# Retention's output projection: gate blocks added by accumulating transfers, output weights split at other places, weight sums copied through another queue

## The chip, the cores and the metric

The kernel runs on one core of one Trainium2 chip. The number that counts is the time of one execution on the device, in microseconds (us), lower is better. Each version is run several times and the median is taken; one more execution is recorded by the hardware profiler. The engines are called PE (TensorE: matmuls, with PEld for its weight loads), DVE (VectorE), ACT (ScalarE), POOL (GpSimd) and SP (SyncE, which here only issues transfers).

## The reference

One layer of a hybrid diffusion backbone on 1024 latent tokens of width 1024, with 256 context tokens. An input projection feeds a neighbourhood attention and a bidirectional retention; both are projected back, merged by sigmoid gates, projected once more, and a gated MLP with a depthwise convolution follows. What matters here:

```python
def _merge(o_na, o_ret, gate_na, gate_ret, w_proj_na, w_proj_ret, w_out):
    merged = jax.nn.sigmoid(gate_na) * (o_na @ w_proj_na) + jax.nn.sigmoid(gate_ret) * (o_ret @ w_proj_ret)
    return merged @ w_out
...
        x = x + g1 * _merge(o_na, o_ret, xga, xgb, w_proj_na[l], w_proj_ret[l], w_out[l])
        hx2 = _modulate(_rmsnorm(x, norm2_g[l]), sh2, sc2)
        x = x + g2 * _conv_ffn(hx2, w_up[l], conv_w[l], conv_b[l], w_down[l])
```

All numbers are fp32. w_up has 1024 x 5632 numbers, w_down 2816 x 1024.

## The kernel before

**Products.** An fp32 product is made of three matmuls on reduced-precision operands. Each operand is split into a high part, a copy by ACT (L95), and a low part, a subtraction by DVE (L96): what `split` does. A "block" is 128 x 512 numbers. Large products go by a scheme with seven products of half-size matrices in place of eight (`Seven`), for which sums and differences of weight blocks are needed. `block_sums` (L555) makes them ahead of time in DRAM: for each job four copies from DRAM to DRAM (`copy_of`, L562 in the profile) and four transfers that add onto the destination (`sum_of`, through `add`, L558 in the profile). All are issued by POOL, a few at a time: `puts` lets POOL read one number of a given tile, so that it waits for a place in the work, and then issues the next n items. Sums that were not made ahead (for up's units from `PRE` on) are made by POOL when the unit is loaded: four additions of two blocks, L1431 to L1434 in `Seven.load`.

**Stages**, in the profiled execution: attention to 400 us; retention 400 to 738 (a loop over heads and chunks, `slot`); gate products 738 to 891; the retention's projection 891 to 975; output tiles 975 to 1077; the opening of up 1077 to 1140; up with its convolution to 1500; down to the end. Most of the order is chosen by a scheduler that ships with the language. Written by hand are the parts inside `tc.manual_schedule()`, and single instructions fixed to their place by `late`. All engines work through their own instructions in order.

**The projection** (L1791 on) runs over q = 0 to 27: seven products p of four column blocks n, q = 4p + n, 12 matmuls each. In step q the program issues loads (weights two steps ahead with `w_load`, operands `x_load`, output weights `wo_load`, old products and gates `merge_load`), the block's matmuls, the evacuation of block q - 1, the splitting of weights for q + 2 (`w_split`, tile wc), of operands (`x_split`, tile xop), of output weights (tiles wo, wx or wc), and merges. A finished block is multiplied by its gate on DVE (`merged`, L1717), and POOL adds the other branch's gated product (L1718), which SP loaded from d_pn into a tile of its own. `merge` then splits the sum into mh (ACT) and ml (DVE); for the first row half in steps 10 to 13 and 18 to 21, for the second in the loop over output tiles.

**The output tiles**: `out_proj(tb)` for eight row blocks tb, each two halves dh of 48 matmuls with the split weights `wo[kb, dh]` (eight blocks kb), evacuated by DVE in two instructions (L1844, L1845), then normalized. In the projection's steps 2 to 9 the eight weight blocks of dh = 0 were split, in steps 24 to 27 six of dh = 1; two more follow behind it.

**SP's queue** has eight lanes; a transfer waits, by a semaphore of the program, until the one eight places ahead has landed. POOL's transfers go through its own queue.

Of the kernel before, what the change touches and what calls it, by code (L numbers as in the profile page):

```python
# [40 lines left out]
def tile_hybrid_layer(ctx, tc: tile.TileContext, io, dbg=None):  # L41
# [510 lines left out]
    NH, EARLY, PRE = NF // 2, 4, 4  # L552
    seq = [j + NH * i for j in range(NH) for i in range(2)]

    def block_sums(jobs):  # L555
# [4 lines left out]
        def copy_of(n, c):  # L560
            d, x, y, z, w = jobs[n]
            late(pool.dma_start(d[c], (y, z, z, w)[c]))  # L562
# [750 lines left out]
    def slot(main, mix, head=None, i=None):  # L1313
# [57 lines left out]
    for it in (tl, gate_sums):  # L1371
# [277 lines left out]
    def w_load(p, n):  # L1649
# [5 lines left out]
        if n % 2 == 0 or (p, n) == (0, 1):  # L1655
# [12 lines left out]
    for n, (i, k) in enumerate(steps):  # L1668
        gu[i].step(k)
        if k in (1, 2, 3):  # L1670
            puts(pret_sums if n < 40 else up_sums, (gu[i].u3 if k == 3 else gu[i].u2)[:, 0:1], 2)
        if n in marks:
# [5 lines left out]
            for n_ in {4: (0, 1), 5: (2,)}.get(m, ()):  # L1678
# [26 lines left out]
    def merge_load(db, half):  # L1705
        sg[db, half] = t = [gtile(half, F32, "sg") for _ in range(2)]
        sync.dma_start(t[0], d_pn[db, half])
        sync.dma_start(t[1], d_gate[2 * db + 1, half])

    def merge_gate(db, half):  # L1710
        t = sg[db, half][1]
# [3 lines left out]
    def merged(db, half, src):  # L1715
        s_, g = sg[db, half]
        vec.tensor_tensor(g, src, g, ALU.mult)  # L1717
        pool.tensor_tensor(g, g, s_, ALU.add)  # L1718
# [3 lines left out]
    def merge(db, half):  # L1722
        g = sg[db, half][1]
        mg[db, half] = h_, l_ = gtile(half, F32R, "mh"), gtile(half, F32R, "ml")
        split(h_, l_, g)
# [3 lines left out]
    def wo_load(kb, dh=0):  # L1729
        woraw[kb, dh] = raw = gtile(1, F32, "wr") if dh == 0 else wpool.tile([P, 512], F32, tag="raw", bufs=3, name="raw")  # L1730
        sync.dma_start(raw, io["w_out"][dh, kb])

    def wo_split(kb, dh=0):
        if dh == 0:
            wo[kb, dh] = t = wop.tile([P, 2, 512], F32R, tag="wo", bufs=KB, name="wo")
        else:
            wo[kb, dh] = t = wop.tile([P, 2, 512], F32R, tag="wx", bufs=2, name="wx") if kb >= 6 else wtile()
        split(t[:, 0], t[:, 1], woraw.pop((kb, dh)))
# [7 lines left out]
    WO = {2 + kb: kb for kb in range(KB)}  # L1746
    WX = {24: (6,), 25: (7,), 26: (0, 1), 27: (2, 3)}
    WX_LOAD = {22: (6,), 23: (7,), 24: (0, 1), 25: (2,), 26: (3,)}
    NQ = 7 * KH

    def loads(q):
        if q in XS:
            x_load(*XS[q], lambda: gtile(1, F32, "xr"))
        if 3 <= q + 2 < NQ:
            w_load(*divmod(q + 2, KH))
        if q in WO:
            wo_load(WO[q])

# [32 lines left out]
    with tc.manual_schedule():  # L1791
        for q in (1, 2):
            loads(q)
        for q in range(NQ + 1):
# [4 lines left out]
            for kb in WX_LOAD.get(q, ()):  # L1799
                wo_load(kb, 1)  # L1800
# [10 lines left out]
            if q in WO:  # L1811
                wo_split(WO[q])
            for kb in WX.get(q, ()):
                wo_split(kb, 1)
# [3 lines left out]
            for q0, b in ((10, 0), (18, KH)):  # L1818
# [13 lines left out]
    def out_proj(tb):  # L1832
        half, ts = tb // 4, slice((tb % 4) * P, (tb % 4 + 1) * P)
        x1 = op.tile([P, D], F32, tag="x1", bufs=3, name="x1")
        xr = op.tile([P, D], F32, tag="xn", bufs=2, name="xn")
        sync.dma_start(x1, io["x"][tb * P : (tb + 1) * P])
        for dh in range(2):
            cs = slice(dh * 512, dh * 512 + 512)
            m = po.tile([P, 512], F32, tag="o", bufs=2, name="om")
            for kb in range(KB):  # L1840
                wc = wo[kb, dh]
                h_, l_ = mg[kb, half]
                mm3(m, h_[:, ts], l_[:, ts], wc[:, 0], wc[:, 1], kb == 0, kb == KB - 1)
            vec.tensor_tensor(xr[:, cs], m, gate1[:, cs], ALU.mult)  # L1844
            vec.tensor_tensor(x1[:, cs], xr[:, cs], x1[:, cs], ALU.add)  # L1845
# [6 lines left out]
        return xr  # L1852

# [215 lines left out]
    with tc.manual_schedule():  # L2069
        for kb in (4, 5):  # L2070
# [415 lines left out]
```

## Time and profile before

| what | value |
|---|---|
| median of three runs | 1724.77 us (1721.01 to 1727.42) |
| profiled execution | 1728.52 us, of which the span 1726.8 us |
| PE busy in the span | 1695.7 us, 98% |
| DVE / ACT / POOL busy | 74% / 49% / 37% |
| mean granted clock of PE | 0.995 |
| transfers | 346.11 MB, mean 200 GB/s |

The span runs from the first to the last instruction of the profile; the execution's own time has a little around it. A matmul counts as busy while it is in the pipeline, so PE's share is no measure of how near it is to its best; the number of matmuls in a stretch says more. The rows of the page that show where time is spent evenly and where not (40 slices of 43.2 us each; 9 is 90% or more):

```profile
PE   9999999999999999999999899999999999999998
DVE  5777786665877877567569956798899998846756
POOL 2112234323344333024322321056666666421444
DMA  9256779853352533899988566856766776998744
```

PE dips below nine tenths in the 23rd slice (950 to 993 us); DVE is at nine tenths there and in the slice before.

### The profile page before, as it was taken

The numbers are of one execution on the slowest core, as the hardware profiler recorded it, in microseconds if no ns is written. First come the engines' busy times: TensorE is split into PE (matmuls) and PEld (weight loads), VectorE is DVE, ScalarE is ACT, GpSimd is POOL, SyncE is SP. The second block draws the span as 40 slices with busy tenths as digits, with TensorE's granted clock in tenths as the row PEclk, the third lists the DMA queues.
The fourth block names the chain that finished last, engine by engine and source line by source line (L and its number), as shares of the span: only waits on it lengthen the run. The fifth ranks groups of instructions, "written<-read, shape, count | busy, mean of one in ns | idle before, by whom it ended". The sixth has DMA issues, their size and how long they took to land.

```text
span 1726.8 us, 25317 instructions
## 1 busy us (share of the span) xinstructions
PE 1695.7 (98%) x8365; PEld 1414.2 (82%) x8365; DVE 1283.1 (74%) x2481; ACT 842.0 (49%) x1777; POOL 633.2 (37%) x805
## 2 busy tenths in 40 slices
PE   9999999999999999999999899999999999999998
PEld 7788888888888887888888687778888888888886
DVE  5777786665877877567569956798899998846756
ACT  6565665553453444443455433644444444544444
POOL 2112234323344333024322321056666666421444
PEclk9999999999999999999999999999999999999999
DMA  9256779853352533899988566856766776998744
GB/s 378 92 152 161 179 199 240 202 129 91 81 157 79 171 62 109 286 305 333 281 255 305 181 204 192 286 166 193 194 171 173 197 203 167 266 316 287 244 155 175
DMA packets 168451, 346.11 MB, mean 200 GB/s; under 512 B 29952, under 2 KB 46880, under 8 KB 161728
## 3 DMA queue, kind: packets, MB, share of 16 engines
q1 hardware_dynamic: 132464, 243.45, 41.6%
q0 software_dynamic: 21248, 86.10, 23.2%
q10 hardware_dynamic: 14608, 14.95, 2.5%
q8 instruction: 66, 1.08, 0.2%
q14 instruction: 65, 0.53, 0.1%
HBM read 268.08 MB, written 141.87 MB: 237 GB/s over the span
## 4 chain that ended last, share of the span: by engine, by line
PE 50%; DVE 6%; issue 6%; POOL 3%; DMA 3%; ACT 1%; SPq 0%; POOLq 0%; DVEq 0%; ACTq 0%
PE u L1422 30%; PE y L1422 3%; PE pr L1422 2%; PE mm L132 1%; PE mm L131 1%; PE mm L130 1%; DVE wc L96 1%; PE om L130 1%; PE om L132 1%; PE om L131 1%; DMA ur<-d_a 1%; PE pn L119 1%; PE pn L120 1%; PE pn L121 1%; PE mm L1422 1%
## 5 line engine op out<-in xcount | busy, mean ns | idle before, releaser
L1422 PE MATMUL u<-T,wc 128*128 128x512 f32 x1056 | 248.0, 391 | 3.5 <-DVE pu L1469 3.3
L1422 PEld LDWEIGHTS u<-T,wc 128*128 128x128 f32 x1056 | 199.1, 189 | 46.2 <-issue 2.6
L1422 PE MATMUL y<-wc,ahl 128*128 128x512 f32 (+1 forms) x936 | 210.4, 387 | 0.7 <-DVE wc L96 0.7
L1422 PEld LDWEIGHTS y<-wc,ahl 128*128 128x128 f32 x936 | 174.1, 188 | 37.0 <-DVE wc L96 1.4
L96 DVE TENSOR_TENSOR wc<-ur,wc 128x512 fp32r<-128x512 f32 x155 | 118.1, 765 | 45.6 <-ACT wc L95 43.8
L95 ACT CAST wc<-ur 128x512 fp32r<-128x512 f32 x155 | 95.5, 621 | 92.1 <-PE y L1422 44.9
L1422 PE MATMUL u<-h2a,wc 128*128 128x512 f32 x504 | 118.6, 390 | 1.1 <-ACT pu L1930 1.1
L120 PE MATMUL mm<-low,wc 128*128 128x512 f32 (+1 forms) x312 | 119.2, 382 | 0.0
L1422 PEld LDWEIGHTS u<-h2a,wc 128*128 128x128 f32 x504 | 94.8, 188 | 21.1 <-ACT pu L1930 1.5
L534 POOL DMA_DIRECT2D d_ona<-rs x32 | 32.7, 1023 | 208.7 <-DVE st L495 65.5
L119 PE MATMUL mm<-hx,wc 128*128 128x512 f32 x264 | 107.4, 407 | 0.3 <-ACT hc L233 0.3
L121 PE MATMUL mm<-hx,wc 128*128 128x512 f32 x264 | 105.0, 398 | 0.0
L1422 PE MATMUL u<-hxT,wc 128*128 128x512 f32 x384 | 90.0, 389 | 0.0
L95 ACT CAST wc<-s 128x512 fp32r<-128x512 f32 x72 | 44.8, 622 | 85.7 <-PE u L1422 83.5
L1422 PEld LDWEIGHTS u<-hxT,wc 128*128 128x128 f32 x384 | 72.1, 188 | 14.9
L593 POOL COPY pad<-pu 128x1 f32<-128x1 f32 x62 | 39.3, 633 | 91.9 <-DVE pu L1463 76.8
L96 DVE TENSOR_TENSOR wc<-s,wc 128x512 fp32r<-128x512 f32 x72 | 69.3, 963 | 0.7 <-ACT wc L95 0.3
L96 DVE TENSOR_TENSOR ahl<-ur,ahl 128x512 fp32r<-128x512 f32 x66 | 52.5, 802 | 23.2 <-ACT ahl L95 22.9
L132 PE MATMUL mm<-wc,low 128*128 128x512 f32 (+1 forms) x180 | 68.9, 383 | 0.0
L95 ACT CAST wc<-wr 128x512 fp32r<-128x512 f32 x69 | 42.5, 619 | 53.3 <-PE u L1422 39.4
L1422 PE MATMUL pr<-xop,wc 128*128 128x512 f32 x264 | 63.4, 399 | 4.6 <-DVE xop L96 2.9
L120 PEld LDWEIGHTS mm<-low,wc 128*128 128x128 f32 x312 | 59.2, 190 | 7.2
(441 smaller groups left out, 4724.5 us busy)
## 6 DMA issues: line engine op xcount, KB each, us to landing
ur<-in_w_up SPq DMA_DIRECT2D x80, 256.0 KB, 5.2
d_a<-at SPq DMA_DIRECT2D x77, 256.0 KB, 3.1
ur<-d_a SPq DMA_DIRECT2D x77, 256.0 KB, 5.3
d_w<-in_w_down POOLq DMA_DIRECT2D x66, 256.0 KB, 7.3
aw<-in_w_ada SPq DMA_DIRECT2D x32, 512.0 KB, 4.4
d_a<-d_a POOLq DMA_DIRECT2D x44, 256.0 KB, 7.3
ur<-d_w SPq DMA_DIRECT2D x44, 256.0 KB, 3.6
ur<-in_w_down SPq DMA_DIRECT2D x33, 256.0 KB, 5.5
```

What stands on the lines that cost most here:

```text
L95: act.copy(hi, src)
L96: (lo_eng or vec).tensor_tensor(lo, src, hi.bitcast(F32), ALU.subtract)
L119: pe.matmul(out, wh, xh, start=k == 0, stop=False)
L120: pe.matmul(out, wh, xl, start=False, stop=False)
L121: pe.matmul(out, wl, xh, start=False, stop=k == n - 1)
L130: pe.matmul(out, ah, bh, start=first, stop=False)
L131: pe.matmul(out, ah, bl, start=False, stop=False)
L132: pe.matmul(out, al, bh, start=False, stop=last)
L534: late(pool.dma_start(o, self.rs[HD:P], accum_op=ALU.add))
L593: late(pool.tensor_copy(tick, src))
L1422: pe.matmul(out, a, b, start=first and n == 0, stop=last and n == 2, skip_group_check=True)
```

## The change

Five things are done.

1. `block_sums`: the copies are issued by SP's queue; the accumulating transfers stay on POOL.
2. The sums of the retention projection's weights (d_p) are issued in the retention, one item in each slot, in place of the gate products; those of up (d_s) take all places of the gate products. `PRE` goes from 4 to 8, so eight of up's units get sums in DRAM and load seven blocks each.
3. `merged` adds the old product with a transfer from d_pn that accumulates into the gate's tile, issued by POOL. The separate load of d_pn is gone. Merges of the first half move two steps later; merges of the second half are fixed to their place in the loop over output tiles, in the order of blocks 4 to 7, then 0 to 3.
4. First-half output weights are split in steps 1 to 5 and 25 to 27. All second-half ones are split behind the first and second output products, which now run as (tile 0, first half), (tile 1, first half), then the second halves of both.
5. One weight block of the first product is loaded earlier, and all four of them go to the same kind of buffer.

The diff, cut to its core:

```diff
-    NH, EARLY, PRE = NF // 2, 4, 4
+    NH, EARLY, PRE = NF // 2, 4, 8
...
         def copy_of(n, c):
-            late(pool.dma_start(d[c], (y, z, z, w)[c]))
+            late(sync.dma_start(d[c], (y, z, z, w)[c]))
...
                     puts(gate_sums, head.r0[i][:, 1, 0:1], n)
+                next(pret_sums, None)
...
-            puts(pret_sums if n < 40 else up_sums, (gu[i].u3 if k == 3 else gu[i].u2)[:, 0:1], 2)
+            puts(up_sums, (gu[i].u3 if k == 3 else gu[i].u2)[:, 0:1], 2)
...
     def merge_load(db, half):
-        sg[db, half] = t = [gtile(half, F32, "sg") for _ in range(2)]
-        sync.dma_start(t[0], d_pn[db, half])
-        sync.dma_start(t[1], d_gate[2 * db + 1, half])
+        sg[db, half] = t = gtile(half, F32, "sg")
+        sync.dma_start(t, d_gate[2 * db + 1, half])
...
     def merged(db, half, src):
         vec.tensor_tensor(g, src, g, ALU.mult)
-        pool.tensor_tensor(g, g, s_, ALU.add)
+        pool.dma_start(g, d_pn[db, half], accum_op=ALU.add, max_dma_last_dim=8192)
...
-    WO = {2 + kb: kb for kb in range(KB)}
-    WX = {24: (6,), 25: (7,), 26: (0, 1), 27: (2, 3)}
+    WO = {1: (0,), 2: (1,), 3: (2,), 4: (3,), 5: (4,), 25: (5,), 26: (6,), 27: (7,)}
...
-            for q0, b in ((10, 0), (18, KH)):
+            for q0, b in ((12, 0), (20, KH)):
                 if 0 <= q - q0 < KH:
                     merge(b + q - q0, 0)
...
+        out_begin(1)
+        evacuated(NQ - 1)
...
+        m = out_mm(0, 0)
+        for kb in range(5):
+            wx_split(kb)
+        out_evac(0, 0, m)
+        m = out_mm(1, 0)
+        for kb in range(5, KB):
+            wx_split(kb)
+        out_evac(1, 0, m)
+        for tb in (0, 1):
+            out_half(tb, 1)
...
-        for kb in range(2 * tb, min(2 * tb + 2, KB)):
+        for kb in ((4, 5), (6, 7), (0, 1), (2, 3))[tb] if tb < KH else ():
             merge(kb, 1)
```

`out_begin`, `out_mm`, `out_evac` and `out_end` are the pieces of the former `out_proj`; for tiles 2 to 7 they run in the former order.

**DVE at the end of the projection.** Before, in the last four steps (L96 is the low part of a split, L1788 the evacuation, L1717 the multiplication by the gate):

```order
L96 TENSOR_TENSOR wc<-raw,wc 128x512
L96 TENSOR_TENSOR wx<-raw,wx 128x512
L1788 TENSOR_TENSOR u_10435<-u_10435,pr 128x512
L1717 TENSOR_TENSOR sg<-u_10435,sg 128x512
L96 TENSOR_TENSOR wc<-wr,wc 128x512
L96 TENSOR_TENSOR wx<-raw,wx 128x512
L1788 TENSOR_TENSOR u_10468<-u_10468,pr 128x512
L1717 TENSOR_TENSOR sg<-u_10468,sg 128x512
L96 TENSOR_TENSOR wc<-raw,wc 128x512 x2
L1788 TENSOR_TENSOR u_10501<-u_10501,pr 128x512
L96 TENSOR_TENSOR ml<-sg,mh 128x512
L1717 TENSOR_TENSOR sg<-u_10501,sg 128x512
```

After, from step 25 to the first output tile's evacuation (there L1785 is the evacuation, L1846 the output tile's):

```order
L1785 TENSOR_TENSOR u_10497<-u_10497,pr 128x512
L1717 TENSOR_TENSOR sg<-u_10497,sg 128x512
L96 TENSOR_TENSOR wo<-wr,wo 128x512
L1785 TENSOR_TENSOR u_10525<-u_10525,pr 128x512
L1717 TENSOR_TENSOR sg<-u_10525,sg 128x512
L96 TENSOR_TENSOR wo<-wr,wo 128x512
L1785 TENSOR_TENSOR u_10552<-u_10552,pr 128x512
L1717 TENSOR_TENSOR sg<-u_10552,sg 128x512
L96 TENSOR_TENSOR wc<-raw,wc 128x512 x3
L96 TENSOR_TENSOR wc<-wr,wc 128x512
L96 TENSOR_TENSOR wx<-wr,wx 128x512
L1846 TENSOR_TENSOR xn<-om,gate_10306 128x512
```

The splits of second-half output weights (wx, wc from raw) stood among the last evacuations and now stand behind the last; merges of the second half (ml) are gone from this place.

**POOL at the start of up.** Before, with the sums of an up unit:

```order
L2053 TENSOR_TENSOR zs<-zs,pu 128x512 x2
L1431 TENSOR_TENSOR s<-ur 128x512
L1432 TENSOR_TENSOR s<-s,ur 128x512
L1433 TENSOR_TENSOR s<-ur 128x512
L1434 TENSOR_TENSOR s<-ur,s 128x512
L593 COPY pad<-pu 128x1
L562 DMA d_w<-in_w_down 16x4096 x2
L1981 DMA d_a<-d_a 32x2048
```

After, where the first such sums stand several units later, among the accumulating transfers for down:

```order
L558 DMA d_w<-in_w_down 32x2048
L1993 DMA d_a<-d_a 32x2048
L593 COPY pad<-pu 128x1
L558 DMA d_w<-d_w 32x2048
L1993 DMA d_a<-d_a 32x2048
L593 COPY pad<-pu 128x1
L558 DMA d_w<-in_w_down 32x2048
L1993 DMA d_a<-d_a 32x2048
L1432 TENSOR_TENSOR s<-ur 128x512
L1433 TENSOR_TENSOR s<-s,ur 128x512
```

Four units' sums are gone from POOL's row, and the copies for down (L562) with them.

**SP in the gate products.** Before, loads of gate weights (wr) and of the projection's (raw):

```order
L1508 DMA wr<-in_w_rg 128x512
L1508 DMA wr<-d_g 128x512 x2
L1533 DMA o<-d_oret 128x512 x2
L1508 DMA wr<-d_g 128x512
L1508 DMA wr<-in_w_rg 128x512 x2
```

After, at the same place, with copies of up's weight blocks (L562) among them:

```order
L1509 DMA wr<-in_w_rg 128x512
L1509 DMA wr<-d_g 128x512 x2
L562 DMA d_s<-in_w_up 16x4096 x4
L1534 DMA o<-d_oret 128x512
L562 DMA d_s<-in_w_up 16x4096
L1534 DMA o<-d_oret 128x512
L562 DMA d_s<-in_w_up 16x4096 x2
L1509 DMA wr<-d_g 128x512
L1509 DMA wr<-in_w_rg 128x512
```

Seven copies went in between two weight loads here.

More of the change, by code (lines that the diff above doesn't have):

```diff
@@ L1793, in tile_hybrid_layer @@
             loads(q)
-        for q in range(NQ + 1):
+        for q in range(NQ):
             for q0, b, half in ((5, 0, 0), (13, KH, 0), (18, KH, 1), (23, 0, 1)):
@@ L1810, in tile_hybrid_layer @@
                 x_split(*XS[q])
[L1811 to L1814, printed above, removed]
+            for kb in WO.get(q, ()):
+                wo_split(kb)
             for q0, half in ((8, 0), (24, 1)):
@@ L1852, in out_proj @@
         return xr
+    def out_proj(tb):
+        if tb > 1:
+            out_begin(tb)
+            for dh in range(2):
+                out_half(tb, dh)
+        return out_end(tb)
     vos = {}
```

86 lines of the change are left out of this document (47 added, 39 removed).

## The prediction

> **What bounds the kernel now.** I read the page first: TensorE (PE) is busy 98% of the span, so a change can pay only where PE is not busy, or busy at a lower clock. The windows of 20 us say where that is (columns: stretch, length, busy time and count of PE, PEld, DVE, ACT, POOL, granted clock, DMA share, GB/s):
>
> ```profile
> 920.00:940.00 20.00, 20.00 (x89) 16.54 (x89) 19.97 (x29) 9.33 (x18) 5.61 (x4) 1.00 0.86 286
> 940.00:960.00 20.00, 18.27 (x79) 14.49 (x78) 19.83 (x23) 8.37 (x15) 8.75 (x6) 1.00 0.52 179
> 960.00:980.00 20.00, 17.11 (x67) 13.32 (x66) 19.72 (x23) 8.21 (x15) 8.53 (x6) 0.91 0.58 182
> 980.00:1000.00 20.00, 17.92 (x71) 13.91 (x70) 13.55 (x21) 5.71 (x10) 4.54 (x6) 0.91 0.68 221
> 1120.00:1140.00 20.00, 20.00 (x90) 16.57 (x89) 19.96 (x25) 13.20 (x17) 1.62 (x1) 1.00 0.66 220
> 1140.00:1160.00 20.00, 17.03 (x74) 13.44 (x72) 19.60 (x20) 6.98 (x10) 17.49 (x12) 1.00 0.47 145
> 1160.00:1180.00 20.00, 19.64 (x80) 16.12 (x81) 19.16 (x20) 8.83 (x12) 13.26 (x13) 0.91 0.63 171
> ```
>
> A full window holds 90 matmuls. The retention projection and the first output tiles (940 to 1000) ran 79, 67 and 71, so 53 are missing; the up projection's start (1140 to 1180) ran 74 and 80, so 26 are missing. In all five VectorE (DVE) is the engine that is full, until the projection ends inside the third. What one matmul is worth comes from the chain of work that ended last, in a stretch without waits:
>
> ```profile
> 891.43 10.88 PE pr L1422 x48
> ```
>
> 10.88 / 48 = 0.2267 us. The first loss is 53 x 0.2267 = **12.0 us**, the second 26 x 0.2267 = **5.9 us**, together 17.9 us. Both hold a dip of the clock: the matmuls that ran slow are counted as missing, so the dip must not be added again.
>
> Why DVE is full there, from the groups of instructions by form, 890 to 1000 us (count | busy us, mean ns):
>
> ```profile
> L1718 POOL TENSOR_TENSOR sg<-sg 128x512 f32<-128x512 f32 x16 | 26.2, 1636 | 63.0 <-DVE sg L1717 33.1 <-DMA xr<-d_rt 24.1 <-DMA wr<-d_p 2.0
> L96 DVE TENSOR_TENSOR xop<-xr,xop 128x512 fp32r<-128x512 f32 x16 | 19.6, 1228 | 0.0
> L96 DVE TENSOR_TENSOR ml<-sg,mh 128x512 fp32r<-128x512 f32 x16 | 14.0, 888 | 0.2
> L96 DVE TENSOR_TENSOR wc<-raw,wc 128x512 fp32r<-128x512 f32 x18 | 13.2, 744 | 2.3 <-ACT wc L95 2.3
> L96 DVE TENSOR_TENSOR wc<-wr,wc 128x512 fp32r<-128x512 f32 x13 | 8.9, 683 | 2.1 <-ACT wc L95 1.8 <-DMA raw<-in_w_pret 0.3
> L96 DVE TENSOR_TENSOR wx<-raw,wx 128x512 fp32r<-128x512 f32 x4 | 6.0, 1503 | 0.0
> L96 DVE TENSOR_TENSOR xop<-row,xop 128x512 fp32r<-128x512 f32 x4 | 3.8, 960 | 0.0
> ```
>
> One subtraction of this shape takes 0.68 us where nothing disturbs it (wc from wr), and up to 1.50 on average elsewhere. The timeline shows beside what (start, length, instruction, idle before it):
>
> ```profile
> 962.11 0.68 DVE L96 TENSOR_TENSOR wc<-wr,wc 128x512 fp32r<-128x512 f32 x1
> 962.33 1.59 POOL L1718 TENSOR_TENSOR sg<-sg 128x512 f32<-128x512 f32 x1 [2.01 <-DVE sg L1717]
> 962.71 1.76 DVE L96 TENSOR_TENSOR xop<-xr,xop 128x512 fp32r<-128x512 f32 x1
> 964.52 7.83 PE L1422 MATMUL pr<-xop,wc 128*128 128x512 f32 x26 [2.63 <-DVE xop L96]
> ```
>
> The subtraction that meets POOL's addition L1718 ends about when that does plus its own time, and PE has by then waited 2.63 us. Summed over the groups, the time above 0.68 us is 8.8 (xop from xr), 3.3 (ml), 1.2 (wc from raw), 3.3 (wx) and 1.1 (xop from row): **17.7 us of stretch**, for 16 additions.
>
> **The change part by part.** The sum goes against the profiled execution (1728.52 us, span 1726.8), which lies 3.75 us above the median of the three runs, 1724.77; I carry the difference over to the median.
>
> *The projection.* Windows by stage, in the columns above:
>
> ```profile
> 400.00:738.00 338.00, 336.81 (x1725) 285.70 (x1724) 244.33 (x743) 150.80 (x403) 115.24 (x181) 1.00 0.47 134
> 738.00:891.00 153.00, 153.00 (x675) 126.45 (x674) 95.07 (x148) 63.59 (x106) 51.98 (x95) 1.00 0.90 286
> 891.00:988.00 97.00, 90.67 (x386) 72.89 (x385) 89.00 (x116) 50.49 (x92) 26.73 (x17) 0.98 0.78 270
> ```
>
> DVE has 89.0 us of work, PE 28 blocks of 12 matmuls, 28 x 12 x 0.2267 = 76.2 us: DVE is the bound by about what is lost. The change takes away POOL's additions, with them 17.7 us, and 17 instructions from DVE's row ahead of the first output tile's evacuation (eight splits of the output weights' second half, one of the first, eight splits of merged rows of half 1; five of the output splits come back behind the last block), 17 x 0.68 = 11.6 us. Left for the blocks are 89.0 - 17.7 - 11.6 = 59.7 us, 78% of PE's 76.2. The last blocks, densest before, have five instructions each (3.4 us at 0.68, of 2.72 a block) only while operands of the seventh product are split beside a merge, in the four blocks q = 20 to 23; DVE falls behind there by 4 x 0.7 = 2.7 us, and weights are split two blocks (5.4 us) ahead. So DVE stops being the bound.
>
> What comes in its place is a wait: ACT's copy into mh now waits for a transfer that adds in DRAM's old product. Between a block's multiply and its merge lie three blocks, 3 x 2.72 = 8.2 us. An accumulating transfer into SBUF does not occur in the trace. The nearest are POOL's copies and additions in DRAM (KB each, median us to landing) and POOL's time for one issue:
>
> ```profile
> d_g<-d_g POOLq DMA_DIRECT2D x16, 256.0 KB, 4.3
> d_a<-d_a POOLq DMA_DIRECT2D x44, 256.0 KB, 7.3
> L558 POOL DMA_DIRECT2D d_s<-d_s x8 | 7.3, 918 | 5.5 <-DMA d_s<-d_s 5.3 <-issue 0.3
> L1058 POOL DMA_DIRECT2D d_b<-low x16 | 21.1, 1431 | 4.5 <-issue 4.5
> L562 POOL DMA_DIRECT2D d_s<-in_w_up x16 | 10.0, 628 | 0.3 <-issue 0.2
> ```
>
> That bounds it between 0.6 + 4.3 = 4.9 and 1.4 + 7.3 = 8.7 us. I take 6.5, the middle. Even 8.7 is only 0.5 late, and behind the waiting copy on ACT stand weight splits that PE needs two blocks later; with DVE 2.7 us behind they have 5.4 - 2.7 = 2.7 us to spare. The wait costs PE nothing up to 8.2 + 2.7 = 10.9 us. Also gone are 16 loads of d_pn from SP's queue.
>
> The second half's eight output splits now stand behind tile (0,0). The product after the first two tiles needs them 48 x 0.2267 = 10.9 us after the first began, and each takes ACT 0.62 and DVE 0.68, so eight take some 5.4, or 8.7 us with the two tiles' four instructions of evacuation (2.8) and a start delay of 0.5; hidden. If that cover failed, the wait would be 1 to 3 us. I leave **0.8 us** for the seam, where before 1.9 us of wait was. Projection: **-12.0 + 0.8 = -11.2** (bounds: -12.0, and -4.8 if the stretch stays, below).
>
> *The start of up.*
>
> ```profile
> 1139.44 1.27 DVE L1962 SCALAR_TENSOR_TENSOR at<-uu,cw,at 128x1023 f32<-128x1023 f32 x1
> 1140.24 2.22 POOL L1431 TENSOR_TENSOR s<-ur 128x512 f32<-128x512 f32 x1 [15.51 <-DMA ur<-in_w_up]
> 1141.24 2.31 DVE L1963 SCALAR_TENSOR_TENSOR at<-uu,cw,at 128x1023 f32<-128x1023 f32 x1
> ```
>
> The four sums L1431 to L1434 begin at 1140.24, the moment PE begins to lose. With eight units prepared by transfer instead of four, four units' sums, 16 additions of about 2 us, go from POOL, and a convolution step beside them falls from 2.31 towards 1.27. DVE was full from 1120 already with PE at x90, so it keeps up narrowly without them: I take **-5.0** of the 5.9 (bounds 0 and -5.9). The 32 extra transfers in DRAM run while up's weights are not yet wanted.
>
> *Retention.* It gets pret's 16 accumulating issues (0.92 us each, 14.7 us) on a POOL busy 115 of 338 us, and loses the issue of 16 gate copies there. PE's dependence on POOL in that stage is small:
>
> ```profile
> PE Q L131 <- POOL SS L1231: 1.0, 4, 0.5
> ```
>
> If every added issue delayed a product by its whole length, that would be 14.7 us; if none, 0. PE waited four times, 0.5 us at the longest, so I stay near the lower end: **+0.5**.
>
> *Gate stage and later.* SP issues the copies, which leaves bytes and destinations as they were; PE is at 153.00 of 153.00 there. I take 0 (bounds 0 and the +24 below).
>
> **Sum:** -11.2 - 5.0 + 0.5 = -15.7; 1728.5 - 15.7 = 1712.8 for a profiled execution, and 1724.77 - 15.7 = **1709 us** for the median.
>
> **The rivals.**
>
> *The stretch stays.* A POOL transfer needs POOL to write it out, and if that slowed DVE as the addition did, 17.7 us would stay and only 11.6 of 29.3 go: 12.0 x 0.40 = 4.8 instead of 11.2, so **1715**. Against it:
>
> ```profile
> 1053.22 0.82 POOL L558 DMA_DIRECT2D d_s<-in_w_up  x1
> 1053.36 0.68 DVE L1886 TENSOR_TENSOR vo<-vo,v 128x512 f32<-128x512 f32 x1
> ```
>
> A DVE addition inside such an issue takes its 0.68.
>
> *Late accumulation.* Landing after 10.9 us in the two groups of merges (q = 12 to 15, 20 to 23) would stop ACT, the weight splits behind it and PE. By the wait of 2.63 above and the dip behind it, granted clock 0.91 over the 20 us at 960, so 0.09 x 20 = 1.8 us, a group costs 4.4:
>
> ```profile
> 966.00:968.00 2.00, 2.00 (x6) 1.53 (x6) 2.00 (x2) 0.00 (x0) 1.53 (x1) 0.50 0.26 61
> ```
>
> (In these 2 us behind the wait the clock was 0.50 and 6 matmuls ran.) Two groups: 1709 + 8.8 = **1718**. For it: landings reach 7.3 as a median, with a DMA share of 0.86 at 920 to 940. The Trainium skill ("SBUF — State Buffer", section "SBUF: two separate sides") gives a rule against this change: a transfer issued from GpSimd's queue starves while VectorE runs an operation that holds the port pair both share, and the advice is to issue it from another engine's queue. By it the accumulates would land later and this rival would hold. Its section "Who interferes with whom" counts a tensor_tensor as not doing so, by inference; the 0.68 beside 0.82 above agrees, and I leave the chance where the rows put it. On the dip the skill ("TensorE: Matmul & The Clock Gate", section "What's actually happening") says the clock halves after an idle window of about 3.4 us; here it was 0.50 behind 2.63 us, so the measurement decides; by the page the rival would cost 2 x 2.6 and give 1714.
>
> *Up stays bound by DVE.* DVE was full at 1120 to 1140 without POOL. If the added load of transfers or DVE's own order keeps PE waiting, the 5.0 is not had: 1709 + 5 = **1714**.
>
> *SP's queue becomes serial*, slower than before. The program lets SP have eight transfers under way, each waiting for its predecessor in the same lane. A copy in DRAM takes about 7 us:
>
> ```profile
> d_p<-in_w_pret POOLq DMA_DIRECT2D x24, 256.0 KB, 7.0
> ```
>
> So it costs the queue 7.0 / 8 = 0.9 us, and the 27 copies that SP gets in the gate stage 24 us, ahead of weight loads that PE needs; the DMA share is 0.90 there already. It decides once SP is behind by more than the loads' lead, some 6 us. Then 1709 + 24 = **1733**. Against it: PE waits for nothing there, and the loads are issued early.
>
> **Chances.** Forecast 1709: 0.60; stretch 1715: 0.07; late accumulation 1718: 0.13; up at 1714: 0.12; SP 1733: 0.08. The range takes in all of the 17.9 us with 4 us of other waits and 3 us of spread (the runs shown lie within 4 us of their median), so 1700, and above it the rivals but SP's: **1700 to 1722**. Within 0.5%, about what a measurement of this kernel can tell from no change, is 1716.1 to 1733.4: faster 0.77, same 0.17 (two thirds of late accumulation, a fourth of the others, a fourth of SP's), slower 0.06.
>
> **What would show it.** Right: windows of x90 from 940 to 1000; no L1718 addition on POOL, and xop's and ml's splits near 0.68; DVE below 80% of the projection; ACT's mh waiting for the transfer under 3 us and PE not at all; no L1431 sums before about 1215, and the clock at 1.00. Wrong: PE waiting for mh's or wc's splits behind that transfer (late accumulation), splits of 1.7 beside POOL's issues (the stretch), PE or ACT waiting for wr or raw at 738 to 891 (SP), DVE at 20 of 20 with PE under x85 at 1140 to 1180 (up). A loss in retention over 2 us would break the term of 0.5.

## The result and the profile after

The changed kernel takes **1711.83 us** (median of four runs, 1710.48 to 1713.06), the kernel before 1724.09 in the runs beside it (1721.01 to 1727.42): a ratio of **0.9928, interval 0.9907 to 0.9950**. The profiled execution took 1713.02 us, its span is 1710.8 us.

First the windows that showed the losses, in the changed kernel (columns as in the prediction):

```profile
940.00:960.00 20.00, 20.00 (x90) 16.57 (x89) 18.29 (x30) 9.37 (x17) 6.08 (x7) 1.00 0.96 233
960.00:980.00 20.00, 20.00 (x90) 16.53 (x90) 15.71 (x26) 6.75 (x11) 4.35 (x5) 1.00 1.06 303
980.00:1000.00 20.00, 20.00 (x93) 16.55 (x92) 13.38 (x29) 7.90 (x16) 4.58 (x7) 1.00 0.65 176
1060.00:1080.00 20.00, 20.00 (x97) 16.67 (x96) 17.17 (x39) 12.02 (x28) 0.54 (x1) 1.00 0.77 266
1080.00:1100.00 20.00, 19.80 (x87) 16.07 (x86) 15.71 (x25) 15.97 (x30) 1.62 (x1) 1.00 0.89 302
1140.00:1160.00 20.00, 20.00 (x90) 16.57 (x89) 15.43 (x20) 9.77 (x15) 3.59 (x5) 1.00 0.87 222
1160.00:1180.00 20.00, 20.00 (x90) 16.55 (x89) 14.49 (x18) 9.23 (x13) 4.67 (x6) 1.00 0.80 220
1520.00:1540.00 20.00, 18.54 (x82) 15.02 (x80) 4.86 (x8) 5.42 (x11) 3.13 (x4) 1.00 0.64 149
1540.00:1560.00 20.00, 15.89 (x60) 12.64 (x61) 12.76 (x19) 11.65 (x21) 3.72 (x4) 0.83 0.98 345
```

Both losses are gone: 90 matmuls and more in every window from 940 to 1000 and from 1140 to 1180, at full clock. And a new one has come, where in the kernel before the windows from 1520 to 1560 held 90: at the start of the down projection 8 + 30 = 38 matmuls are missing, 38 x 0.2267 = 8.6 us. The waits of PE name it; three lines of all of them in the changed kernel (who waits, for whom, us in total, times, longest), the last two from the retention:

```profile
PE y L1423 <- ACT wc L95: 5.6, 1, 5.6
...
PE Q L131 <- POOL SS L1231: 1.2, 4, 0.5
PE dS L132 <- DVE kz L1200: 1.0, 2, 0.6
```

The groups of the projection, 884 to 992 us, changed kernel:

```profile
L1718 POOL DMA_DIRECT2D sg<-d_pn x16 | 14.0, 874 | 62.2 <-DVE sg L1717 30.8 <-DVE wc L96 14.2 <-issue 13.6
...
L96 DVE TENSOR_TENSOR xop<-xr,xop 128x512 fp32r<-128x512 f32 x16 | 10.9, 684 | 0.0
```

The split of xop is back at 0.684 us from 1.228, beside POOL issues of 0.87 us. The window of the whole projection shows that VectorE is no longer the bound, with 60.99 of 77 us:

```profile
891.00:968.00 77.00, 77.00 (x342) 63.75 (x341) 60.99 (x97) 41.45 (x78) 12.81 (x15) 1.00 0.97 290
```

To compare whole stages I use the start of the first matmul of each. For instance, the down projection's, from the view of the tile y (ns shortest/median/longest, first and last start), ahead the kernel before:

```profile
L1422 PE MATMUL y<-wc,ahl x936: 278/389/497, 1507.5 to 1718.3; 128*128 128x512 f32 x183, 128*128 128x256 f32 x5
```

and after:

```profile
L1423 PE MATMUL y<-wc,ahl x936: 277/389/792, 1484.0 to 1702.4; 128*128 128x512 f32 x183, 128*128 128x256 f32 x5
```

PE comes to the down projection 23.5 us earlier and takes 7.6 us longer over it. All kernels of this study in the same manner, us from first matmul to first matmul (down: first to last start), one profile each, with the ratio to the kernel before and its interval:

| kernel | retention | gates | projection | output tiles | up | down | median | ratio |
|---|---|---|---|---|---|---|---|---|
| before | 308.7 | 149.6 | 83.6 | 100.6 | 432.0 | 210.8 | 1724.09 | |
| before, second profile (e9) | 309.0 | 149.6 | 82.0 | 98.0 | 430.4 | 210.1 | 1723.97 | 0.9991 [0.9973, 1.0009] |
| accumulation alone (e7) | 309.1 | 149.6 | 76.2 | 103.1 | 429.1 | 210.3 | 1722.11 | 0.9996 [0.9983, 1.0010] |
| output weights alone (e10) | 309.2 | 149.6 | 81.5 | 96.6 | 431.0 | 210.3 | 1719.30 | 0.9969 [0.9953, 0.9986] |
| both edits of the projection (e11) | 309.5 | 149.6 | 76.1 | 94.7 | 429.4 | 210.9 | 1712.91 | 0.9927 [0.9905, 0.9950] |
| ... and copies on SP (e5) | 307.5 | 149.6 | 76.2 | 94.7 | 427.4 | 217.9 | 1717.83 | 0.9970 [0.9958, 0.9981] |
| ... and pret sums in retention (e4) | 310.9 | 149.6 | 76.1 | 94.7 | 426.7 | 215.7 | 1717.06 | 0.9960 [0.9945, 0.9976] |
| ... and eight units: the change | 310.8 | 149.6 | 76.1 | 94.8 | 420.8 | 218.4 | 1711.83 | 0.9928 [0.9907, 0.9950] |
| the change, down's copies on POOL (e1) | 310.3 | 149.6 | 76.1 | 94.7 | 420.8 | 210.3 | 1704.65 | 0.9898 [0.9877, 0.9919] |

From e11 to the change each row adds one edit to the row above ("pret sums" are the weight sums of the retention projection). Two things limit how finely the table can be read. Each stage time is from one profile: the two profiles of the kernel before differ by up to 2.6 us in a stage, and the four kernels whose retention is the same (the change, e1, e4 and e6) take 310.8, 310.3, 310.9 and 312.0 us for it. And the medians were not all measured side by side: the kernel before, measured beside each group of runs, had medians from 1722.67 to 1724.93 us.

### The profile page after: what moved, and what is told of

It reads as the page before. It is cut to its first block, busy times and chain, and to the rows that moved or that the text cites. A ratio compares the mean times of both kernels' runs of the same rounds, so it can differ in the third digit from the quotient of the medians.

```text
span 1710.8 us, 25367 instructions
## 1 busy us (share of the span) xinstructions
PE 1689.3 (99%) x8365; PEld 1410.8 (82%) x8365; DVE 1256.1 (73%) x2481; ACT 843.3 (49%) x1777; POOL 551.9 (32%) x697
## 5 line engine op out<-in xcount | busy, mean ns | idle before, releaser
L96 DVE TENSOR_TENSOR wc<-ur,wc 128x512 fp32r<-128x512 f32 x171 | 128.4, 755 | 46.1 <-ACT wc L95 44.4
L95 ACT CAST wc<-ur 128x512 fp32r<-128x512 f32 x171 | 105.5, 621 | 105.5 <-PE u L1423 53.8
L96 DVE TENSOR_TENSOR ahl<-ur,ahl 128x512 fp32r<-128x512 f32 x66 | 52.5, 801 | 33.0 <-ACT ahl L95 32.9
L95 ACT CAST wc<-s 128x512 fp32r<-128x512 f32 x56 | 34.8, 622 | 68.6 <-PE u L1423 66.4
L95 ACT CAST wc<-raw 128x512 fp32r<-128x512 f32 x77 | 47.9, 622 | 36.5 <-PE u L1423 5.6
L1423 PE MATMUL u<-hx,wc 128*128 128x512 f32 x192 | 62.3, 390 | 0.0
```

The source lines that it names most:

```text
L95: act.copy(hi, src)
L96: (lo_eng or vec).tensor_tensor(lo, src, hi.bitcast(F32), ALU.subtract)
L1423: pe.matmul(out, a, b, start=first and n == 0, stop=last and n == 2, skip_group_check=True)
```

## The experiments

**e1: only down's copies on POOL again.** The new loss stands at the start of down. The chain behind it in the changed kernel, first POOL's timeline (start, length, instruction, idle before):

```profile
1496.04 0.77 POOL L558 DMA_DIRECT2D d_w<-in_w_down  x1 [6.83 <-DMA d_w<-in_w_down]
1496.62 0.98 POOL L558 DMA_DIRECT2D d_w<-d_w  x1
1508.94 0.77 POOL L558 DMA_DIRECT2D d_w<-in_w_down  x1 [11.34 <-DMA d_w<-in_w_down]
1509.66 0.86 POOL L558 DMA_DIRECT2D d_w<-d_w  x1
1517.76 0.78 POOL L558 DMA_DIRECT2D d_w<-d_w  x1 [7.23 <-DMA ur<-d_a]
1518.42 0.92 POOL L1993 DMA_DIRECT2D d_a<-d_a  x1
1525.13 2.36 POOL L1993 DMA_DIRECT2D d_a<-d_a  x3 [5.79 <-DMA d_a<-d_a]
1536.36 0.77 POOL L1993 DMA_DIRECT2D d_a<-d_a  x1 [8.87 <-DMA d_a<-d_a]
```

then SP's:

```profile
1499.02 1.61 SPq L1986 DMA_DIRECT2D d_a<-at  x3
1502.16 3.06 SPq L562 DMA_DIRECT2D d_w<-in_w_down  x3
...
1540.16 0.32 SPq L2147 DMA_DIRECT2D ur<-d_a  x1
```

The last three copies of down's weights stand on SP behind the stores of up's last activations (d_a from at), and these in turn behind loads of down's first operands (ur). VectorE had made those activations by 1493.3; what came late was SP itself. One of the loads waited 4.8 us, until 1491.63, for an earlier store of activations to land, and the last stores waited 2.0 us for another load to land (`gate<-d_ada`). So the stores go out at 1499 and the copies at 1502. POOL's additions onto them wait 11.3 us, the sums of activations (L1993) stand behind those additions on POOL, and the operands that PE needs are sums of that kind: SP can load the next one at 1540, ACT has then waited 14.3 us for it and splits it ahead of the weights wc, and PE starts again at 1544.09.

```diff
-    def block_sums(jobs):
+    def block_sums(jobs, eng=sync):
...
-            late(sync.dma_start(d[c], (y, z, z, w)[c]))
+            late(eng.dma_start(d[c], (y, z, z, w)[c]))
...
-    dn_sums = block_sums(down_jobs(0, NH))
+    dn_sums = block_sums(down_jobs(0, NH), pool)
```

> The changed kernel, with only the copies of down's weight sums issued by POOL again; all other copies stay on SP. Theory 1 (those copies stand on SP behind the stores of up's last blocks, POOL's additions wait for them, and the activation sums behind these come late): the 5.6 us wait of PE at the start of down goes, the stretch from the first to the last matmul of down takes 211 us in place of 218.4, and the time is about 1704 (7.6 us less than 1711.8). Rival (PE only arrives there 23 us earlier and the activation sums are late by themselves): the wait stays at 4 to 6 us and the time at 1711 to 1713.

Measured: 1704.65 us (1703.38 to 1706.77), the down stage 210.3 us, and the wait is gone. POOL's timeline of e1 at the same place:

```profile
1504.80 0.77 POOL L558 DMA_DIRECT2D d_w<-d_w  x1 [7.76 <-DMA d_w<-d_w]
1505.48 0.88 POOL L1993 DMA_DIRECT2D d_a<-d_a  x1
1512.92 2.36 POOL L1993 DMA_DIRECT2D d_a<-d_a  x3 [6.56 <-DMA d_a<-d_a]
```

The activation sums go out 13 us earlier (1505.48 against 1518.42), though PE comes to the stage only 0.9 us earlier. The rival, that PE only got there too soon, falls: it got there as soon here. This is the fastest version of the study, faster than both kernels.

**e2: all copies on POOL again.** One line, `sync` back to `pool` in `copy_of`.

> The changed kernel, with all copies of the weight sums issued by POOL as before. Theory 1: as in the run with down's copies alone, about 1704, with no loss elsewhere, since the copies on SP gave nothing. Rival (copies on SP are what lets POOL get up's and the projection's sums out in time): PE waits come back at 440 to 480, 1060 to 1100 or 1140 to 1180, each 2 to 6 us, and the time is 1706 to 1712.

Measured: 1710.26 us (1708.29 to 1712.52), ratio 0.9927 [0.9907, 0.9947]. Down takes 210.2 us, as theory 1 has it, but the rival has the time: 5.6 us more than e1. The waits of 2 to 6 us that it named do not appear; no wait of PE in e2 is above 1.4 us. By stages retention takes 312.6 (e1 310.3) and up 423.0 (420.8), 4.5 us together. The stage ahead of retention took 3.7 us more in this profile; since the kernel before and e7, e10 and e11 issue the gate copies there from POOL too and start retention at 431.5 to 433.0 us (e2: 435.3), that part is not put down to the copies. From e11 to e5, where the copies move the other way, retention and up give 2.0 us each. Retention alone would prove little (e6, with its copies on SP, takes 312.0), but the two pairs and the times agree: copies on SP pay in retention and up, and cost in one place, at down.

**e3: the projection's sums among the gate products again.**

```diff
-                next(pret_sums, None)
...
-    for it in (tl, gate_sums, pret_sums):
+    for it in (tl, gate_sums):
...
-            puts(up_sums, (gu[i].u3 if k == 3 else gu[i].u2)[:, 0:1], 2)
+            puts(pret_sums if n < 40 else up_sums, (gu[i].u3 if k == 3 else gu[i].u2)[:, 0:1], 2)
```

> The changed kernel, with the projection's weight sums issued among the gate products again, so that up's sums come later. Theory 2 (issuing them in the retention costs its 2.1 us, and up's earlier sums are what freed the transfers in the output tiles, where the losses at 1060 to 1100 went): retention is back at 308.7 us from the first query product to the first gate product, but the losses at 1060 to 1100 return, 4 to 10 us, and the time is 1714 to 1720. Rival (those losses went because VectorE was relieved): only the 2.1 us change, 1709 to 1710.

Measured: **1741.21 us** (1738.08 to 1743.99), ratio 1.0106 [1.0084, 1.0127], slower than before. Retention falls to 307.5 us, 3.3 less, but up takes 453.2. Neither theory had this. The waits of e3, 1060 to 1130 us:

```profile
ACT T L95 <- DMA ur<-d_t: 29.3, 5, 18.5
POOL d_s L558 <- DMA d_s<-d_s: 26.7, 4, 7.6
...
PE u L1422 <- ACT pu L1941: 19.7, 1, 19.7
```

Eight units' sums no longer get done before up begins: POOL is still issuing up's additions at 1119 us (in the changed kernel the last was at 1043.69). On SP fourteen copies for them stand in one row from 1071.86 to 1087.01, and the load of `d_t` that ACT waits for comes behind them, at 1088.24. So the edits hang together: eight prepared units need the place that the projection's sums leave. The question of the losses at 1060 to 1100 stayed open.

**e4: four units prepared, as before.** `PRE` from 8 to 4.

> The changed kernel, with four units of up prepared by transfer as before, so that POOL makes the sums of units 5 to 8 again. Theory 3 (POOL's sums slow VectorE at the start of up): the windows at 1140 to 1180 lose 20 to 26 of 180 matmuls again, 4.5 to 6 us, and the time is 1716 to 1718. Rival (VectorE is free enough there by now, since it does not lag from the stages before): no loss, 1711 to 1713; in that case fewer transfers may even give 1 us less.

Measured: 1717.06 us (1716.57 to 1717.92), 5.2 more than the change. The loss is back, 20 us earlier on the axis; windows of e4:

```profile
1120.00:1140.00 20.00, 18.89 (x84) 15.21 (x82) 19.89 (x20) 7.74 (x11) 15.91 (x9) 1.00 0.54 182
1140.00:1160.00 20.00, 16.68 (x68) 13.53 (x68) 18.78 (x19) 8.36 (x11) 10.28 (x10) 0.91 0.59 159
```

6 + 22 = 28 missing, and up takes 426.7 in place of 420.8: 5.9 us, a dip of the clock (0.91 over 20 us, 1.8 us) among it. VectorE's splits of up's weights (wc from ur) over 1110 to 1180 us show the stretch: 844 ns on average in the kernel before, 683 in the changed kernel, 906 in e4. Theory 3 holds. POOL's sums of the later units, which in the changed kernel begin at 1184, cost nothing that the windows show: VectorE is busy for 17 to 18.6 of every 20 us there, and PE runs without a gap.

**e5: as e3, with four units.** Both lines of e3 and e4.

> The changed kernel, with the projection's weight sums among the gate products and only four units of up prepared, so both as before; the new projection stays. It separates what e3 mixed. Theory 2 (the losses at 1060 to 1100 come from up's sums crowding the transfers of the output tiles): the two windows at 1060 to 1100 miss 20 to 30 of some 185 matmuls as before, and from the first output product to the first of down it takes 530 us or more (532.6 before, 515.6 after); time 1716 to 1722. Rival (VectorE's relief removed them): the two windows stay within 5 of the changed kernel's, only the 5.9 us of the four units come back, less 3.3 in retention; time 1713 to 1715.

Measured: 1717.83 us (1715.56 to 1721.29). The time lies where theory 2 put it, the windows do not:

```profile
1060.00:1080.00 20.00, 18.53 (x87) 14.67 (x86) 16.16 (x36) 12.49 (x30) 2.20 (x3) 1.00 0.92 289
1080.00:1100.00 20.00, 19.68 (x87) 15.84 (x86) 15.75 (x25) 15.10 (x29) 1.61 (x1) 1.00 0.95 309
```

The same windows in the first profile of the kernel before:

```profile
1060.00:1080.00 20.00, 17.93 (x86) 14.41 (x86) 10.87 (x23) 6.00 (x15) 0.56 (x1) 1.00 0.54 192
1080.00:1100.00 20.00, 16.41 (x67) 12.63 (x66) 14.91 (x35) 13.26 (x30) 2.21 (x3) 0.91 0.91 293
```

87 and 87 matmuls in e5, where the changed kernel has 97 and 87 and the kernel before 86 and 67. That is neither theory 2's 20 to 30 missing nor within the rival's 5. From the first output product to the first of down it is 94.7 + 427.4 = 522.1 us, far from 530. So up's late sums cost little there (0.7 us against e4, 427.4 to 426.7), and theory 2 falls. The time comes from the down stage instead: 217.9 us, the loss of e1, since copies are on SP here too.

**e6: POOL's addition back in the changed kernel**, with SP's second load and its tile (`merge_load` and `merged` as before).

> The changed kernel, with POOL's addition of two tiles (and the second load of SP) in place of the accumulating transfer; output weights stay split where the change put them. Theory 4 (the addition's stretch of VectorE is the larger cause): VectorE has 59.7 + 17.7 = 77.4 us for 76.2 of products, projection and first tiles lose 4 to 8 us again, projection 80 to 84 us from its first product to the first output product; time 1716 to 1719. Rival (moving the splits alone gives VectorE room enough, since the stretch falls where nothing is late): projection 76 to 77 us, time 1711 to 1713.

Measured: 1719.37 us (1717.05 to 1720.56), 7.5 more than the change; the projection takes 82.5 us. The waits of PE in e6:

```profile
PE pr L1423 <- DVE xop L96: 3.2, 1, 3.2
```

and VectorE beside POOL's addition (start, length, instruction, idle before):

```profile
968.75 1.65 POOL L1719 TENSOR_TENSOR sg<-sg 128x512 f32<-128x512 f32 x1 [0.63 <-DVE sg L1718]
969.20 1.76 DVE L96 TENSOR_TENSOR wo<-wr,wo 128x512 fp32r<-128x512 f32 x1
```

Theory 4 holds: without the accumulating transfer the split of xop is what PE waits for, as before. The stretch goes with the addition in every kernel: the sixteen splits of xop from xr take 1228 or 1229 ns on average in both profiles of the kernel before, in e10 and in e6, and 684 in e7, e11 and the changed kernel. SP's second load comes and goes together with the addition, and no run parts the two; the stretched splits say that the addition is what counts.

**e7: the accumulating transfer alone, in the kernel before** (and its merges two steps later).

```diff
-        sync.dma_start(t[0], d_pn[db, half])
...
-        pool.tensor_tensor(g, g, s_, ALU.add)
+        pool.dma_start(g, d_pn[db, half], accum_op=ALU.add, max_dma_last_dim=8192)
...
-            for q0, b in ((10, 0), (18, KH)):
+            for q0, b in ((12, 0), (20, KH)):
```

> The kernel before, with the accumulating transfer in place of POOL's addition alone, and the merges two steps later that go with it; everything else as before. Theory 4: VectorE has 89.0 - 17.7 = 71.3 us for 76.2 of products, so the projection takes 76 to 78 us in place of 83.6, and the time is 1715 to 1719. Rival (the output weights' splits at the end are the cause): 82 to 84 us, time 1722 to 1725.

Measured: 1722.11 us (1719.60 to 1725.66), ratio 0.9996 [0.9983, 1.0010]: no gain. Theory 4 had the stage right, 76.2 us, and the time wrong. The output tiles take 103.1 us, and the waits of e7 from 960 to 995 us say why:

```profile
ACT mh L95 <- DMA sg<-d_pn: 11.2, 4, 6.7
DVE ml L96 <- ACT mh L95: 9.4, 4, 6.5
...
PE om L130 <- DVE xn L1843: 6.3, 1, 6.3
```

In the kernel before, the scheduler had put the second half's merges at the end of the projection, right behind the blocks that feed them. With an addition on POOL that was short; with a transfer ACT and VectorE stand waiting for it, the first output tile's evacuation stands behind them, and PE waits for its bank. The wait that the prediction feared in the first half's merges came in the second half's. That fixing these merges later is what removes it follows from this chain; no run moves the merges without the splits of the output weights.

**e8: e1 with the projection's sums not before the second head.**

```diff
-                next(pret_sums, None)
+                if head.h:
+                    next(pret_sums, None)
```

> The changed kernel with down's copies on POOL (as e1) and the projection's sums not begun before the second head of the retention; the last eight items then come together at its end. Theory 5 (the 1.5 to 2 us lost in retention lie at 440 to 480, where the first of these sums meet the first head): retention 308 to 309 us, time 1702 to 1703.5. Rival (each issue costs its part wherever it stands): retention 310 to 311 us, time 1704 to 1705; or the burst at the end delays gate products, 1706.

Measured: 1706.02 us (1704.72 to 1706.58), no better than e1; retention takes 312.0 us, where theory 5 had 308 to 309. The loss at 440 to 480 (100 and 100 matmuls in the changed kernel, 106 and 106 here) is gone, as theory 5 said, and one at least as large stands at the end, where the last eight items, all at once, meet the loads of the other branch's products (DMA share 1.04; the changed kernel has 90 and 88 matmuls in the last two windows). Windows of e8:

```profile
460.00:480.00 20.00, 20.00 (x106) 16.96 (x106) 15.55 (x54) 7.42 (x23) 7.96 (x14) 1.00 0.21 42
700.00:720.00 20.00, 18.50 (x81) 14.77 (x80) 9.34 (x15) 5.47 (x11) 2.05 (x3) 1.00 1.04 323
720.00:740.00 20.00, 18.64 (x81) 14.50 (x80) 14.72 (x24) 13.29 (x25) 0.00 (x0) 1.00 0.94 316
```

**e9: the kernel before, once more**, for a second profile.

> The kernel before, unchanged, for a second profile of it: its times spread over 1717 to 1728 us, those of the changed kernel over 1710 to 1713. Theory 6 (which of VectorE's late instructions meets one of POOL's additions differs from one execution to the next, so the losses at 940 to 1180 do): projection, output tiles and up differ from the first profile by 2 to 6 us in sum, all other stages by under 1. Rival: the stages before 891 us differ.

Measured: 1723.97 us (1719.08 to 1727.06); the profiled execution took 1720.80, where the first took 1728.52. Projection, output tiles and up differ by 1.6 + 2.6 + 1.6 = 5.8 of those 7.7 us, so the losses do change size from one execution to the next; another 1.5 us lie before the retention. But theory 6 has the reason wrong, in the projection at least. VectorE's stretched splits are the same in both profiles (xop 1228 ns, ml 888), and so are PE's waits for them (2.9 us in two, the longest 2.6). What differs is the clock behind these waits. The window that the prediction shows with 67 matmuls at 0.91 looks like this here:

```profile
960.00:980.00 20.00, 17.36 (x76) 14.04 (x76) 19.72 (x24) 8.62 (x15) 8.23 (x5) 1.00 0.59 187
```

From 940 to 1180 us the first profile has four windows of 20 us at 0.91 (from 960, 980, 1080 and 1160), the second has one (from 1140). At 0.09 x 20 = 1.8 us each, three dips fewer are some 5.4 us, an estimate, of the 5.8.

**e10: the output weights alone**: the change without its accumulation (as e6), copies, four units and the place of the projection's sums as before.

> The kernel before, with the output weights' splits, the first two output tiles and the second half's merges as in the changed kernel, but POOL's additions, the weight sums, their copies and four prepared units as before. Theory 7 (neither of the projection's two edits pays alone: the accumulation alone gave nothing, e7, since VectorE's surplus moved behind the projection, and the output weights alone leave the stretch): projection 81 to 84 us, output tiles 95 us, time 1718 to 1722. Rival (the output weights are the whole of it): projection 76 to 78 us, time 1712 to 1715.

Measured: 1719.30 us (1714.72 to 1724.45), ratio 0.9969 [0.9953, 0.9986], some 5 us: theory 7 in its time and stages, though this edit pays a part by itself. VectorE is nearly as full in the projection of e10 as before (18.80 of 20 us, 19.72 there):

```profile
960.00:980.00 20.00, 17.34 (x69) 14.19 (x70) 18.80 (x25) 8.29 (x14) 9.54 (x6) 0.91 0.79 263
```

**e11: both edits of the projection**, e10 with the transfer. Both runs also have the fifth item of the change, which no run tests alone.

> As e10 with the accumulating transfer too, so both edits of the projection and nothing of the weight sums. Theory 7: projection 76 us, output tiles 95 us, up 427 us, down 210 to 211 us (copies on POOL), time 1713 to 1716. Rival (the copies on SP gave part of what e5 showed): output tiles or up longer by 3 us or more, time 1717 to 1720.

Measured: **1712.91 us** (1710.54 to 1715.60), ratio 0.9927 [0.9905, 0.9950], the whole of the change's gain. Alone they give 0.6 (inside its interval) and 5 us, together 12.

**e12: e1 with the projection's sums two at a time in the middle heads.**

```diff
-                next(pret_sums, None)
+                if head.h in (1, 2):
+                    next(pret_sums, None), next(pret_sums, None)
```

> The changed kernel with down's copies on POOL (as e1) and the projection's sums two at a time in the second and third head of the retention. Theory 5 as e8 left it (at 440 to 480 nothing is lost without them, the loss of e8 was the burst of eight at the end): retention 308.5 to 309.5 us, time 1703 to 1704. Rival (every one of the 16 issues costs its 0.2 us wherever it stands): 310 to 311 us, time 1704.5 to 1705.5.

Measured: 1708.41 us (1706.11 to 1709.23), worse than both expectations; retention takes 313.6 us. The loss stands where the pairs do: PE runs 103 and 98 matmuls from 560 to 600 us, 115 and 106 in e8. So these pairs cost more than single issues, and neither "only the first head" nor "the same wherever" describes it. The change's own spacing, one per slot from the start, was better than this one; against e8's (1706.02 to its 1704.65) no difference is clear.

## Why the prediction was right, and where it was not

The time (1711.83) lies in the range and 3 us above the forecast of 1709; the direction and most of the size are right. That it came so close is partly luck: up gave some 5 us more than forecast, and down lost 7.6 us that were not forecast at all. Point by point:

- **The projection.** "DVE stops being the bound", with 59.7 us left: measured 60.99, over a window that ends with the projection. "-11.2" for the projection and its seam: projection and output tiles fall from 184.2 us (180.0 in the second profile) to 170.9, so 13.3 or 9.1. e6 and e7 show that POOL's addition, and the stretch it puts on VectorE, is what held the blocks. What the prediction did not see is that the merges of the second half had to be fixed later for this to reach the clock: it counted their eight splits as work saved, but by the waits of e7 their place is a condition.
- **The wait for the transfer.** Taken at 6.5 us between 4.9 and 8.7; the issue list of the changed kernel has, in KB and median us to landing:

```profile
sg<-d_pn POOLq DMA_DIRECT2D x16, 256.0 KB, 7.0
```

  The 10.9 us of cover were enough: PE waits nowhere in the projection. "ACT's mh waiting under 3 us" was wrong, it waits 14.1 us in eight times, 6.3 at the longest; the splits of weights and operands that stand behind it on ACT still came in time. The rival of late accumulation did not come here (the latest of the sixteen landed after 9.2 us), and a wait of its kind did come in e7. Its price, 4.4 us with a dip of the clock behind a wait of 2.63 us, was one execution's: behind the same wait the second profile has no dip.
- **The stretch stays** (1715): out, by 0.684 us for xop beside issues of 0.87.
- **The start of up**, "-5.0" of 5.9: e4 shows 5.9 in the stage and 5.2 in the time, so term and cause are right. The stage gained more, 431.2 (mean of two profiles) to 420.8; the ladder of e11, e5 and e4 gives the rest: 1.8 with the projection's edits, 2.0 with copies on SP, 0.7 with the projection's sums moved, each no larger than one profile can be off. The prediction listed two losses; the windows from 1060 to 1100 (86 and 67 matmuls) held a third that it did not count. The sign it named, no sums of the later units before about 1215, was off: in the changed kernel they begin at 1184, and cost PE nothing.
- **Retention, "+0.5"**: measured +2.1, and e5 to e4 gives 307.5 to 310.9, 3.4 us for moving 16 additions and their copies there; copies of gate weights off POOL return 2.0 (e11 to e5). By the same code in four kernels the +2.1 could as well be 1.3 to 3.3. The prediction looked at one wait of PE, Q for SS. In none of these profiles is that wait above 1.6 us in all, and with the wait for kz it comes to 2.2 us in the changed kernel, so PE's direct waits show at most two thirds of the loss.
- **"Gate stage and later. SP issues the copies ... I take 0": this step failed.** The bound beside it, 24 us, stood at the wrong stage. The gate stage kept its 149.6 us in every kernel. SP's queue did cost 7.6 us, at the start of down: not by being too slow for what it carries, but because three copies stood behind loads and stores that were themselves waiting for transfers to land. The prediction followed the moved copies through one stage and not through the last.
- **The sum.** -15.7 was made against a profiled execution of 1728.52 and carried to the median unchanged. That execution had more of these very losses than most, four dips of the clock from 940 to 1180 us where the second, of 1720.80, had one. Against the mean of both profiles (last product at 1714.5 against 1702.4) the change gains 12.1 us, as the medians do (12.3). A loss that varies should be sized from more than one execution.

So in the end the projection's two edits carry all of the gain (e11: 1712.91), the three edits around the weight sums come out even (e11 to the change, 1.1 us, inside the spread): eight units give 5.2, copies in retention and up some 4, the projection's sums cost some 3 in retention and the copies at down 7.2. These are differences of single steps, good to some 2 us, and do not add up exactly. With down's copies left on POOL the whole is 1704.65.

What stays open: why pairs of issues in retention (e12) cost more than single ones, what carries the rest of the loss at 440 to 480, and when a short wait of PE is followed by a dip of the clock.

## What to carry to other kernels

When an addition becomes a transfer, look at every instruction that reads its result, and move those that stand close behind it; an edit that looks like tidying (fixing the merges later) can be the condition of the gain. When transfers move to another queue, follow them through every stage in which they are issued, and look for what stands ahead of them there and waits: here three copies behind a few waiting loads and stores cost more than all the copies of the gate stage. Two edits that relieve the same engine may pay only together, so try them in all four combinations before crediting one.

## What the runs showed of the hardware

An accumulating transfer from DRAM into SBUF, 256 KB, landed after 7.0 us as a median and took POOL 0.87 us to issue, while VectorE's subtractions beside it took their 0.68 us. The Trainium skill ("SBUF — State Buffer", section "SBUF: two separate sides") warns that transfers issued by GpSimd starve while VectorE holds the ports that both share; here the landing was the same as that of the additions in DRAM (d_a, 7.0 us), so nothing of it was seen with these subtractions. VectorE is busy beside those too, so the comparison does not exclude a small delay.

PE's clock fell to half during the 5.6 us wait at down, 3.4 us after it began (at 1538.5), and stayed there for some 4.7 us of work behind it (0.50 to 1548, 0.81 in the next window). Windows of 2 us of the changed kernel, PE starting again at 1544.09:

```profile
1542.00:1544.00 2.00, 0.00 (x0) 0.00 (x0) 0.45 (x1) 1.10 (x2) 0.00 (x0) 0.50 1.13 286
1544.00:1546.00 2.00, 1.89 (x4) 1.20 (x5) 0.84 (x2) 0.44 (x2) 0.00 (x0) 0.50 0.94 341
1546.00:1548.00 2.00, 2.00 (x6) 1.56 (x5) 1.67 (x3) 1.78 (x4) 0.00 (x0) 0.50 1.02 377
1548.00:1550.00 2.00, 2.00 (x8) 1.60 (x7) 1.12 (x3) 0.97 (x3) 0.00 (x0) 0.81 1.05 396
```

4.7 us at half the clock are 2.3 us of work lost, so 7.9 of the 8.6 us that the wait costs are the wait and its dip, by this estimate. In the first profile of the kernel before, after the wait of 2.63 us that ended at 964.52, the clock still stood at 0.97 from 964 to 966 and at 0.50 from 966: it fell some 4 us after the wait began, when PE had been at work again for over a microsecond. In the second profile PE waited 2.64 us at the same place, behind the same shorter waits of some 1.2 and 0.3 us, and the clock stayed at 1.00 in every window of 2 us from 950 to 992. So a short wait can be followed by a dip that one does not expect to belong to it, in one execution and not in the next, and here that made most of the difference between the two.
